# Weight sums of seven-product gate and up slices: formed in SBUF by VectorE in place of DRAM, and twelve more slices computed that way

## The chip, the cores and the metric

The kernel runs on one core of a Trainium2 chip. The metric is device time of one execution in microseconds (us); the figure of a kernel is the median of its runs. Engines: PE is TensorE (matmuls), DVE is VectorE, ACT is ScalarE, POOL is GpSimd, SP issues DMAs.

## The reference

The program is one inference step of a two-layer decoder for a prompt group (1024 tokens) and a sample group (8 tokens) with d_model = 1024. Layer 0 mixes with a gated linear recurrence and memory attention, layer 1 with stick-breaking attention over a shared K/V and memory attention. What the change touches is the feed-forward net that ends each layer:

```python
def swiglu(h, w_gu, w_down):
    gate, up = jnp.split(h @ w_gu, 2, axis=-1)
    return (jax.nn.silu(gate) * up) @ w_down
...
        h = h + rmsnorm(mix, g[1])
        h = h + rmsnorm(swiglu(rmsnorm(h, g[2]), w_gu[l], w_down[l]), g[3])
```

`w_gu[l]` is 1024 x 5632 (2816 gate columns, then 2816 up columns), `w_down[l]` is 2816 x 1024. Everything is float32.

## The kernel before, in words

**Halves.** The tokens are worked in two halves: g = 0 has 512 columns (tokens), g = 1 has 520 (512 prompt tokens and the 8 samples). Activations lie transposed, features on partitions. Every weight tile of 128 columns by 512 rows (256 KB) is loaded by SP into a raw tile (`wraw`, 5 buffers), then split in two float32r parts: ACT casts the high part (L260, L542) and DVE subtracts it from the raw tile for the low part (L261, L543), both into one tile of `wspl` (5 buffers). A product takes three matmuls per 128 x 128 block: high by high, high by low, low by high. For g = 1 each matmul covers 260 tokens.

**Feed-forward.** It has 22 slices of 128 gate and 128 up columns, in five parts of 5, 5, 4, 4 and 4 slices (`PARTS`). After the slices of a part come the eight down projections over that part (4 or 5 row blocks each), added up in a tile R. `ffn` (L688) runs three of the four feed-forward nets, among them `f1`, layer 0's second half: per slice two calls of `proj` (L266), one for gate and one for up, each 8 row blocks x 3 matmuls x 2 token halves = 48 matmuls of 260 columns. `proj` takes its PSUM tile from `mmp`, which has two buffers of two banks. SiLU is there built from Exp and Ln (`silu`, L284).

**Seven products.** The last stage of the program is `ffn_w` (L615), layer 1's second half. Its first four slices are plain (`gate_up_q`, L499). The other 18 run through `gate_up_w` (L524): gate and up weights and the two token halves form a 2 x 2 block product, which is computed with seven products of half size in place of eight. A product is 4 row blocks x 3 = 12 matmuls, a slice 84. Three of the seven weights are blocks of `w_gu`; the other four are sums of blocks:

- s1 = a21 + a22, s3 = a11 + a21, s2 = s3 + a22, s4 = s2 + a12 (a11, a12: upper and lower 512 rows of the gate columns; a21, a22: the same of the up columns).

The sums of the token side are formed once by `sums_w` (L326). In a slice, four PSUM tiles pa, pb, pc, pd are chained: product 0 goes to pa, ACT copies its negative to pb (L559); product 1 goes to pd; product 2 adds to pb, ACT copies its negative to pc (L562); product 3 adds to pa (gate of the first half, Silu at L565); product 4 adds to pb, and DVE adds pd's copy to it (L570); product 5 adds to pc, and DVE subtracts (L572); product 6 adds to pb, which is up of the first half. Two multiplications (L575, L576), a cast (L281) and a subtraction (L282) make the slice's `m` tile. In `ffn_w` the PSUM pool `quads` holds two sets of four banks, and `spl` (L624) takes three of every eight split tiles from `cpool` beside `wspl`.

**The sums before.** `weight_sums` (L588) forms s1 to s4 of layer 1 in DRAM, part by part, with 40 DMAs on POOL's queue, 16 of them beside parts 0 and 1 of `f1` and the others beside parts 2 to 4 of `f1`. Each waits for a small copy on ACT (L602) and one on POOL (L603), which tie it to the progress of `f1`. In the last stage each slice loads seven tiles of 256 KB: three from `w_gu`, four from the DRAM sums.

**Order.** The program is written as generators that `weave` interleaves by weights; the tile framework then orders each engine's instructions by its own planning and gives buffers and waits. An engine runs its instructions in that order. `f1`'s parts 0 and 1 are woven with the attention of `b0`; parts 2 to 4 run with the sums alone; then come the output projection of layer 1 (`o0`), the shared K/V, the attention of the second half, and the last stage.

Of the kernel before, what the change touches and what calls it, by code (L numbers as in the profile page):

```python
# [2 lines left out]

# [6 lines left out]
F32 = mybir.dt.float32  # L10
F32R = mybir.dt.float32r
# [7 lines left out]
P = 128  # L19
# [5 lines left out]
def tile_decoder(  # L25
# [46 lines left out]
    def nm(s):  # L72
        uid[0] += 1
        return f"{s}_{uid[0]}"
# [12 lines left out]
    def Q(i):  # L87
        return single[0].tile([P, 512], F32, tag=f"q{i}", name=nm("q"))
# [234 lines left out]
            out.append(x)  # L323
            yield

    def sums_w(xs, ops):  # L326

        n, h = NG[1], PW[1]  # L330
        for k in range(4):
            x0, x1 = xs[k], xs[k + 4]
            y = YT()
            if k % 2 == 0:
                z, u = YT(), YT()
            o = (k % 2) * h

            def full(x, c):
                t = B()
                nc.vector.tensor_add(t[:, :h], x[:, 0, c : c + h].bitcast(F32), x[:, 1, c : c + h].bitcast(F32))  # L340
                return t

            b11, b12, b21, b22 = full(x0, 0), full(x0, h), full(x1, 0), full(x1, h)
            for d, p, a, b in (
                (b11, u[:, :, o : o + h], b12, b11), (b12, y[:, :, h : 2 * h], b12, b22),
                (b22, y[:, :, :h], b22, b11), (b21, z[:, :, o : o + h], b21, b22),
            ):
                nc.vector.tensor_sub(d[:, :h], a[:, :h], b[:, :h])
                split_to((p[:, 0, :], p[:, 1, :]), d[:, :h])
            ops.append([  # L350
                x0[:, :, :h], x1[:, :, :h], x1[:, :, h:n], z[:, :, o : o + h], u[:, :, o : o + h],
                y[:, :, :h], y[:, :, h : 2 * h],
            ])
            yield

    def YT():
        return xpool.tile([P, 2, NG[1]], F32R, tag="x0", name=nm("y"))

    def wo_tiles(g):
# [161 lines left out]
        split_to((mt[:, 0, :n], mt[:, 1, :n]), sg[:, :n])  # L521
        return mt, last

    def gate_up_w(l, f, ops, spl, raws):  # L524

        h, n = PW[1], NG[1]
        part, o = part_of(f)
        gate, up = f * P, DFF + f * P
        src = [
            (w_gu[l][0:512, gate : gate + P], 0), (sums[l][part][0][:, o : o + P], 4), (sums[l][part][1][:, o : o + P], 5),  # L530
            (w_gu[l][512:D, gate : gate + P], 1), (sums[l][part][2][:, o : o + P], 6), (sums[l][part][3][:, o : o + P], 2),
            (w_gu[l][512:D, up : up + P], 3),
        ]

        def weight(j):
            r = raws()
            nc.sync.dma_start(r, src[j][0].rearrange("(k p) m -> p k m", p=P))
            return r.rearrange("p k m -> p (k m)")

        def split(src):  # L540
            w = spl()
            nc.scalar.copy(w[:, 0, :], src)  # L542
            nc.vector.tensor_sub(w[:, 1, :], src, w[:, 0, :].bitcast(F32))  # L543
            return w

        def product(ps, j, first=False):
            w = split(weight(j))
            i = src[j][1]
            for k in range(4):
                x = ops[k][i]  # L550
                for wi, (wj, xi) in enumerate(((0, 0), (0, 1), (1, 0))):
                    nc.tensor.matmul(  # L552
                        ps[:, :h], w[:, wj, k * P : (k + 1) * P], x[:, xi, :],
                        start=(first and k == 0 and wi == 0), stop=(k == 3 and wi == 2), skip_group_check=True,
                    )

        pa, pb, pc, pd = (Q(i) for i in range(4))
        product(pa, 0, True)
        nc.scalar.activation(pb[:, :h], pa[:, :h], AF.Copy, scale=-1.0)  # L559
        product(pd, 1, True)  # L560
        product(pb, 2)
        nc.scalar.activation(pc[:, :h], pb[:, :h], AF.Copy, scale=-1.0)  # L562
        product(pa, 3)
        sg = T()
        nc.scalar.activation(sg[:, :h], pa[:, :h], AF.Silu)  # L565
        product(pb, 4)
        dt = T()
        nc.scalar.copy(dt[:, h:n], pd[:, :h])
        gt = T()
        nc.vector.tensor_add(gt[:, h:n], dt[:, h:n], pb[:, :h])  # L570
        product(pc, 5)
        nc.vector.tensor_sub(gt[:, :h], pc[:, :h], dt[:, h:n])  # L572
        product(pb, 6)
        nc.scalar.activation(sg[:, h:n], gt[:, :h], AF.Silu)
        nc.vector.tensor_mul(sg[:, :h], sg[:, :h], pb[:, :h])  # L575
        nc.vector.tensor_mul(sg[:, h:n], sg[:, h:n], gt[:, h:n])  # L576
        mt = M(F32R)
        split_to((mt[:, 0, :n], mt[:, 1, :n]), sg[:, :n])
        return mt

    sums = {}

    def part_of(f):
        for i, (f0, nf) in enumerate(PARTS):
            if f0 <= f < f0 + nf:
                return i, (f - f0) * P

    def weight_sums(l, parts, after):  # L588

        for i in parts:  # L590
            f0, nf = PARTS[i]
            w = nf * P
            s1, s2, s3, s4 = (tc.dram_tile([512, w], F32, name=nm("wsum")) for _ in range(4))
            sums.setdefault(l, {})[i] = (s1, s2, s3, s4)
            a11, a12 = (w_gu[l][r : r + 512, f0 * P : f0 * P + w] for r in (0, 512))
            a21, a22 = (w_gu[l][r : r + 512, DFF + f0 * P : DFF + f0 * P + w] for r in (0, 512))
            for d, a, add in (
                (s3, a11, False), (s1, a21, False), (s3, a21, True), (s1, a22, True),
                (s2, s3, False), (s2, a22, True), (s4, s2, False), (s4, a12, True),
            ):  # L600
                tok = small([P, 1], tag="rr")
                nc.scalar.copy(tok, after())  # L602
                mark = nc.gpsimd.tensor_copy(small([P, 1], tag="mk", bufs=1), tok)  # L603
                with tc.issue_after(mark.ins):
                    if add:
                        nc.gpsimd.dma_start(d, a, accum_op=ALU.add)
                    else:
                        nc.gpsimd.dma_start(d, a, max_dma_last_dim=4 * w)
                yield

    htok = []

# [2 lines left out]
    class ffn_w:  # L615


        def __init__(self, l, x, plain):
            self.g, self.l, self.x, self.ops, self.plain, self.n, self.r, self.pi = 1, l, x, [], plain, 0, 0, 0
            self.R = self.acc = None  # L620
            self.half = []
            self.sums = sums_w(x, self.ops)

        def spl(self):  # L624
            self.n += 1
# [2 lines left out]
            return wspl.tile([P, 2, 512], F32R, tag="ws", name=nm("ws"))  # L628

        def raws(self):  # L630
            self.r += 1
            if self.pi and self.r % 2:
                if not self.half:
                    t = apool.tile([P, 2, 4, P], F32, tag="a", name=nm("w"))
                    self.half = [t[:, 0], t[:, 1]]
                return self.half.pop(0)
            return wraw.tile([P, 4, P], F32, tag="w", name=nm("w"))

        def part(self, pi):
            l, n, h = self.l, NG[1], PW[1]  # L640
# [3 lines left out]
            for j in range(nf):  # L644
                self.pi = pi
                if f0 + j < self.plain:
                    mt, ins = gate_up_q(l, f0 + j, self.x)
                    mids.append(mt)
                    with tc.issue_after(ins.ins):
                        for _ in range((1, 2, 1, 0)[j]):  # L650
                            next(self.sums, None)
                else:
                    mids.append(gate_up_w(l, f0 + j, self.ops, self.spl, self.raws))
                yield
            if pi == 0:
                self.R = R_one()
# [29 lines left out]
            yield from finish_rows(self)  # L686

    class ffn:  # L688
        def __init__(self, g, l, xt, rows=False):
            self.g, self.l, self.xt, self.rows = g, l, xt, rows  # L690
            self.R = self.acc = None

        def part(self, pi):
            g, l = self.g, self.l
# [2 lines left out]
            last = pi == len(PARTS) - 1  # L697
            mids = []
            for j in range(nf):
                pg = proj(g, w_gu[l], 0, ND, (f0 + j) * P, self.xt)  # L700
                sg = silu(None, pg, g)
                pu = proj(g, w_gu[l], 0, ND, DFF + (f0 + j) * P, self.xt)
# [1 line left out]
                mt = M(F32R)  # L704
                split_to((mt[:, 0, :n], mt[:, 1, :n]), sg[:, :n])
                mids.append(mt)
                self.now = sg[:, 0:1]
                yield
            if pi == 0:
                self.R = R_one()  # L710
            if last:
                self.acc = small([P, WID], tag="st", bufs=3)
            for m in range(ND):
                ps = proj(g, w_down[l], f0, nf, m * P, mids)
                evac_raw(g, self.R, ps, m, self.acc, pi == 0, last)
                self.now = self.R[m][:, 0:1]
                if last and self.rows:
                    nc.scalar.activation(
                        self.R[m][:, :n], self.R[m][:, :n], AF.Copy, scale=gcol(l, 3, m)
# [1 line left out]
                    if m == 3:  # L721
                        first_half(self)
                if m % 2:
                    yield

        def finish(self, store):
# [770 lines left out]
    b0 = mixer_b(0, xb0)  # L1497
    weave((b0.heads(), 8), (o1.finish(), 17))
    b0.open()
    f1 = ffn(1, 0, o1.x)  # L1500
    ws = weight_sums(1, range(5), lambda: f1.now)
    weave((chain(b0.sb(), b0.mem()), 24), (chain(f1.part(0), f1.part(1)), 18), (islice(ws, 16), 17))
    weave((chain(f1.part(2), f1.part(3), f1.part(4)), 24), (ws, 24))
    xk1, xb1 = [], []
    o0 = out_proj(0, 1, M)
    drain(o0.mm(b0.xo, 0, 1))
# [52 lines left out]
```

## Time and profile before

| what | value |
|---|---|
| median of 3 runs | 2497.13 us (2494.14 to 2497.49) |
| profiled execution: its time, its span | 2499.1 us, 2497.4 us |
| DVE, ACT, POOL busy, share of the span | 63%, 47%, 4% |
| DMA on SP's queue, on POOL's queue | 301.08 MB, 54.53 MB |
| TensorE's mean granted clock | 0.997 |

The profile's views are read so: the page gives busy time per engine; the chain of waits follows what ended last back from the end; the windows give each engine's busy time in a stretch; the timeline lists instructions with start and duration in us; groups give the mean of one instruction in ns and what ended the idle time ahead of it. A line number is that of the kernel before.

### The profile page before, as it was taken

The page shows a single profiled execution, that of the slowest core. Times are in us where ns is not written, and L with a number is a line of the kernel's source. Part 1 is how long each engine was busy: PE and PEld are TensorE (multiplying, and loading weights), DVE is VectorE, ACT ScalarE, POOL GpSimd, SP SyncE. Part 2 cuts the span into 40 slices and gives each one's busy share as a digit, 9 for nine tenths or more (in the row PEclk, how much of TensorE's full clock was granted, in tenths as well). Part 3 has the DMA queues.
Part 4 walks back from the last instruction along what each step waited for, and adds up shares of the span by engine and source line. Part 5 has one row for each costly group of instructions (what it writes and reads, how often), then busy time and mean ns, then how long its engine had stood idle before and what let it go on. Part 6 is the DMA issues. An engine that isn't in the chain of part 4 may idle for free.

```text
span 2497.4 us, 40764 instructions
## 1 busy us (share of the span) xinstructions
PE 2462.8 (99%) x15565; PEld 2169.9 (87%) x15565; DVE 1571.8 (63%) x2756; ACT 1183.0 (47%) x2277; POOL 98.3 (4%) x139
## 2 busy tenths in 40 slices
PE   8999999999999999999999999999999999999998
PEld 6888988877877897999999989877787797999997
DVE  5766556655765585655544575777577648755655
ACT  5446543243433454555433454555444445564444
POOL 1000000000000000010111100022000000000000
PEclk9999999999999999999999999999999999999999
DMA  5352252233643447586678976544454234365542
GB/s 186 114 165 68 72 156 81 60 110 116 184 124 98 129 138 227 156 195 177 173 191 215 234 193 196 160 142 138 121 149 130 85 115 122 121 192 145 151 137 69
DMA packets 496110, 358.21 MB, mean 143 GB/s; under 512 B 19110, under 2 KB 443635, under 8 KB 495915
## 3 DMA queue, kind: packets, MB, share of 16 engines
q1 hardware_dynamic: 477354, 301.08, 40.5%
q0 software_dynamic: 18560, 54.53, 9.1%
q8 instruction: 122, 2.00, 0.3%
q14 instruction: 74, 0.60, 0.1%
HBM read 325.73 MB, written 75.94 MB: 161 GB/s over the span
## 4 chain that ended last, share of the span: by engine, by line
PE 88%; DVE 5%; DMA 3%; ACT 2%; issue 2%; POOL 0%; SPq 0%; DVEq 0%; ACTq 0%; POOLq 0%
PE mm L274 59%; PE q L552 7%; PE q L667 5%; PE s L1180 2%; PE q L510 2%; PE mm L1048 2%; PE s L903 1%; PE s L862 1%; PE mm L812 1%; DMA b<-qd 1%; PE mm L839 1%; DVE ws L261 1%; PE ns L957 1%; PE s L1336 1%; DMA c<-in_cache_sb_v,pidx 1%
## 5 line engine op out<-in xcount | busy, mean ns | idle before, releaser
L274 PE MATMUL mm<-x,ws 128*128 128x260 f32 (+1 forms) x7776 | 1332.9, 330 | 0.0
L274 PEld LDWEIGHTS mm<-x,ws 128*128 128x128 f32 x7776 | 1148.3, 188 | 151.5 <-issue 12.0
L260 ACT CAST ws<-w 128x512 fp32r<-128x512 f32 x712 | 420.2, 591 | 763.2 <-PE mm L274 620.2
L261 DVE TENSOR_TENSOR ws<-w,ws 128x512 fp32r<-128x512 f32 x712 | 462.5, 653 | 286.8 <-ACT ws L260 278.3
L274 PE MATMUL mm<-m,ws 128*128 128x512 f32 (+1 forms) x2112 | 393.5, 343 | 0.1
L274 PEld LDWEIGHTS mm<-m,ws 128*128 128x128 f32 x2112 | 324.4, 189 | 49.9 <-issue 2.6
L667 PE MATMUL q<-m,ws 128*128 128x260 f32 x1056 | 128.8, 283 | 0.0
L667 PEld LDWEIGHTS q<-m,ws 128*128 128x128 f32 x1056 | 127.2, 188 | 0.4 <-ACT hT L485 0.2
L543 DVE TENSOR_TENSOR ws<-w,ws 128x512 fp32r<-128x512 f32 x126 | 86.6, 691 | 61.5 <-ACT ws L542 59.3
L552 PE MATMUL q<-y,ws 128*128 128x260 f32 x864 | 112.9, 283 | 0.0
L542 ACT CAST ws<-w 128x512 fp32r<-128x512 f32 x126 | 78.0, 621 | 69.6 <-PE q L667 27.4
L552 PEld LDWEIGHTS q<-y,ws 128*128 128x128 f32 x864 | 107.6, 189 | 0.0
L291 DVE TENSOR_SCALAR t<-mm 128x512 f32<-128x512 f32 (+1 forms) x82 | 56.7, 692 | 79.6 <-PE mm L274 79.6
L447 DVE TENSOR_TENSOR r<-r,mm 128x512 f32<-128x512 f32 (+1 forms) x96 | 66.0, 688 | 61.1 <-PE mm L274 60.3
L703 DVE TENSOR_TENSOR t<-t,mm 128x512 f32<-128x512 f32 (+1 forms) x66 | 45.5, 690 | 74.2 <-PE mm L274 73.9
L295 DVE TENSOR_TENSOR t<-t,t 128x512 f32<-128x512 f32 (+1 forms) x66 | 45.8, 694 | 70.6 <-ACT t L294 70.6
L552 PE MATMUL q<-x,ws 128*128 128x260 f32 x648 | 86.3, 282 | 0.0
L552 PEld LDWEIGHTS q<-x,ws 128*128 128x128 f32 x648 | 81.3, 188 | 0.0
L314 DVE TENSOR_TENSOR st<-st,n 128x512 f32<-128x512 f32 (+1 forms) x98 | 67.1, 691 | 8.8 <-ACT n L313 7.0
L281 ACT CAST m<-t 128x512 fp32r<-128x512 f32 (+1 forms) x88 | 54.9, 624 | 18.1 <-DVE t L703 8.9
L282 DVE TENSOR_TENSOR m<-t,m 128x512 fp32r<-128x512 f32 (+1 forms) x88 | 61.0, 693 | 2.6 <-ACT m L281 1.4
L984 POOL DMA_INDIRECT c<-in_cache_sb_k,pidx x16 | 16.4, 1026 | 1170.5 <-ACT n L313 958.6
(339 smaller groups left out, 2557.9 us busy)
## 6 DMA issues: line engine op xcount, KB each, us to landing
w<-in_w_gu SPq DMA_DIRECT2D x334, 256.0 KB, 3.4
w<-in_w_down SPq DMA_DIRECT2D x160, 256.0 KB, 3.5
w<-in_w_in_a SPq DMA_DIRECT2D x80, 256.0 KB, 3.0
wsum<-in_w_gu POOLq DMA_DIRECT2D x18, 1024.0 KB, 9.5
w<-wsum SPq DMA_DIRECT2D x72, 256.0 KB, 3.8
w<-in_w_o SPq DMA_DIRECT2D x64, 256.0 KB, 2.8
wsum<-in_w_gu POOLq DMA_DIRECT2D x12, 1280.0 KB, 10.7
w<-in_w_mem_kv SPq DMA_DIRECT2D x32, 256.0 KB, 3.2
```

The source lines that it names most:

```text
L260: nc.scalar.copy(ws[:, 0, :n, :], raw[:, :n, :])
L261: nc.vector.tensor_sub(ws[:, 1, :n, :], raw[:, :n, :], ws[:, 0, :n, :].bitcast(F32))
L274: nc.tensor.matmul(ps[:, a, : PW[g]], wt, xt[k][:, xi, o : o + PW[g]], start=(k == 0 and wi == 0), stop=(k == nk - 1 and wi == 2),)
L281: nc.scalar.copy(dst[0], src)
L282: nc.vector.tensor_sub(dst[1], src, dst[0].bitcast(F32))
L291: nc.vector.tensor_scalar(sv(x, g), pv(ps, g), -44.0, None, op0=ALU.max)
L314: nc.vector.tensor_add(acc[:, :n], acc[:, :n], t[:, :n])
L447: nc.vector.tensor_add(dst, dst, pv(ps, g))
L542: nc.scalar.copy(w[:, 0, :], src)
L543: nc.vector.tensor_sub(w[:, 1, :], src, w[:, 0, :].bitcast(F32))
L552: nc.tensor.matmul(ps[:, :h], w[:, wj, k * P : (k + 1) * P], x[:, xi, :], start=(first and k == 0 and wi == 0), stop=(k == 3 and wi == 2), ...
L667: nc.tensor.matmul(pp[a][:, :h], wt, mids[k][:, xi, a * h : (a + 1) * h], start=(k == 0 and wi == 0), stop=(k == nf - 1 and wi == 2),)
```

## The change

The DRAM sums go, with their DMAs and the small copies. A slice loads two tiles of 512 KB, one with all 1024 rows of its gate columns and one with those of its up columns (`sums_here`), and DVE forms the four sums of 128 x 512 in SBUF, into `wraw` tiles. In `ffn_w` the raw tiles come from `apool` (from `cpool` in part 0). In `f1` the slices from 10 on, twelve in parts 2 to 4, run through `gate_up_w` too: raw tiles from `cpool` (4 buffers), split tiles from `wspl` (5), and the four PSUM tiles from the two buffers of `mmp` (pa and pd in one, pb and pc in the other). `sums_w` for them is woven into the down projections of part 1 with tiles of `apool`. Silu needs another ACT table than the rest of that stage, so a table load stands ahead of the first such slice and one behind the last.

```diff
+    def sums_here(l, f, raws, outs):
+        cols = []
+        for m0 in (f * P, DFF + f * P):
+            r = raws()
+            nc.sync.dma_start(
+                r.rearrange("p a (k m) -> p (a k) m", m=P), w_gu[l][:, m0 : m0 + P].rearrange("(k p) m -> p k m", p=P)
+            )
+            cols.append(r)
+        (a11, a12), (a21, a22) = ((r[:, 0, :], r[:, 1, :]) for r in cols)
+        kept = {}
+
+        def add(a, b):
+            t = outs()
+            nc.vector.tensor_add(t, a, b)
+            return t
+
+        def weight(j):
+            if j == 1:
+                return add(a21, a22)
+            if j == 2:
+                kept[3] = add(a11, a21)
+                kept[2] = add(kept[3], a22)
+                return kept[2]
+            if j == 4:
+                return kept[3]
+            if j == 5:
+                return add(kept[2], a12)
+            return (a11, None, None, a12, None, None, a22)[j]
+
+        return weight
+
-    def gate_up_w(l, f, ops, spl, raws):
+    def gate_up_w(weight, ops, spl, quads):
...
-        def weight(j):
-            r = raws()
-            nc.sync.dma_start(r, src[j][0].rearrange("(k p) m -> p k m", p=P))
-            return r.rearrange("p k m -> p (k m)")
...
-        pa, pb, pc, pd = (Q(i) for i in range(4))
+        pa, pb, pc, pd = quads()
...
-    def weight_sums(l, parts, after):
...
     class ffn_w:
...
         def raws(self):
-            self.r += 1
-            if self.pi and self.r % 2:
-                if not self.half:
-                    t = apool.tile([P, 2, 4, P], F32, tag="a", name=nm("w"))
-                    self.half = [t[:, 0], t[:, 1]]
-                return self.half.pop(0)
-            return wraw.tile([P, 4, P], F32, tag="w", name=nm("w"))
+            if self.pi:
+                return apool.tile([P, 2, 512], F32, tag="a", name=nm("w"))
+            return C()
...
     class ffn:
-        def __init__(self, g, l, xt, rows=False):
+        def __init__(self, g, l, xt, rows=False, prod=NF):
...
+            self.sums = sums_w(xt, self.ops, lambda: A(F32R))
+
+        def quads(self):
+            ta, tb = (mmp.tile([P, 2, 512], F32, tag="mm", name=nm("mm")) for _ in range(2))
+            return ta[:, 0, :], tb[:, 0, :], tb[:, 1, :], ta[:, 1, :]
...
             for j in range(nf):
+                if f0 + j >= self.prod:
+                    mt, gate = gate_up_w(
+                        sums_here(l, f0 + j, C, lambda: wraw.tile([P, 512], F32, tag="w", name=nm("w"))),
+                        self.ops, lambda: wspl.tile([P, 2, 512], F32R, tag="ws", name=nm("ws")), self.quads,
+                    )
+                    mids.append(mt)
+                    yield
+                    continue
...
+            if last and self.prod < NF:
+                with tc.issue_after(gate.ins):
+                    nc.scalar.preload_act_table_set("natural_log_exp_and_others")
...
                 if m % 2:
+                    if f0 + nf == self.prod < NF:
+                        next(self.sums, None)
                     yield
...
-    f1 = ffn(1, 0, o1.x)
-    ws = weight_sums(1, range(5), lambda: f1.now)
-    weave((chain(b0.sb(), b0.mem()), 24), (chain(f1.part(0), f1.part(1)), 18), (islice(ws, 16), 17))
-    weave((chain(f1.part(2), f1.part(3), f1.part(4)), 24), (ws, 24))
+    f1 = ffn(1, 0, o1.x, prod=10)
+    weave((chain(b0.sb(), b0.mem()), 24), (chain(f1.part(0), f1.part(1)), 18))
+    drain(f1.part(2), f1.part(3), f1.part(4))
```

More of the change, by code (lines that the diff above doesn't have):

```diff
@@ L1 @@
 from contextlib import ExitStack
-from itertools import islice
 import concourse.bass as bass
@@ L324, in normed, with sums_w @@
             yield
-    def sums_w(xs, ops):
+    def sums_w(xs, ops, YT):
         n, h = NG[1], PW[1]
@@ L354, in sums_w, with Y0 @@
             yield
-    def YT():
+    def Y0():
         return xpool.tile([P, 2, NG[1]], F32R, tag="x0", name=nm("y"))
@@ L522, in gate_up_q @@
         return mt, last
-    def gate_up_w(l, f, ops, spl, raws):
-        h, n = PW[1], NG[1]
[L527 to L533, printed above, removed]
-        def weight(j):
-            r = raws()
-            nc.sync.dma_start(r, src[j][0].rearrange("(k p) m -> p k m", p=P))
-            return r.rearrange("p k m -> p (k m)")
+    def sums_here(l, f, raws, outs):
[26 more added lines that the diff above has]
+    def gate_up_w(weight, ops, spl, quads):
+        h, n = PW[1], NG[1]
+        src = (0, 4, 5, 1, 6, 2, 3)
         def split(src):
@@ L547, in product @@
             w = split(weight(j))
-            i = src[j][1]
+            i = src[j]
             for k in range(4):
@@ L573, in gate_up_w @@
         product(pb, 6)
-        nc.scalar.activation(sg[:, h:n], gt[:, :h], AF.Silu)
+        last = nc.scalar.activation(sg[:, h:n], gt[:, :h], AF.Silu)
         nc.vector.tensor_mul(sg[:, :h], sg[:, :h], pb[:, :h])
@@ L578, in gate_up_w @@
         split_to((mt[:, 0, :n], mt[:, 1, :n]), sg[:, :n])
[L579 to L586, printed above, removed]
-    def weight_sums(l, parts, after):
[L590 to L609, printed above, removed]
+        return mt, last
     htok = []
@@ L618, in __init__ @@
         def __init__(self, l, x, plain):
-            self.g, self.l, self.x, self.ops, self.plain, self.n, self.r, self.pi = 1, l, x, [], plain, 0, 0, 0
+            self.g, self.l, self.x, self.ops, self.plain, self.n, self.pi = 1, l, x, [], plain, 0, 0
             self.R = self.acc = None
-            self.half = []
-            self.sums = sums_w(x, self.ops)
+            self.sums = sums_w(x, self.ops, Y0)
         def spl(self):
@@ L652, in part @@
                 else:
-                    mids.append(gate_up_w(l, f0 + j, self.ops, self.spl, self.raws))
+                    mids.append(gate_up_w(
+                        sums_here(l, f0 + j, self.raws, lambda: wraw.tile([P, 512], F32, tag="w", name=nm("w"))),
+                        self.ops, self.spl, lambda: [Q(i) for i in range(4)]
+                    )[0])
                 yield
@@ L688, in tile_decoder @@
     class ffn:
-        def __init__(self, g, l, xt, rows=False):
-            self.g, self.l, self.xt, self.rows = g, l, xt, rows
+        def __init__(self, g, l, xt, rows=False, prod=NF):
+            self.g, self.l, self.xt, self.rows, self.prod = g, l, xt, rows, prod
             self.R = self.acc = None
+            self.ops = []
+            self.sums = sums_w(xt, self.ops, lambda: A(F32R))
+        def quads(self):
+            ta, tb = (mmp.tile([P, 2, 512], F32, tag="mm", name=nm("mm")) for _ in range(2))
+            return ta[:, 0, :], tb[:, 0, :], tb[:, 1, :], ta[:, 1, :]
         def part(self, pi):
@@ L706, in part @@
                 mids.append(mt)
-                self.now = sg[:, 0:1]
                 yield
+            if last and self.prod < NF:
+                with tc.issue_after(gate.ins):
+                    nc.scalar.preload_act_table_set("natural_log_exp_and_others")
             if pi == 0:
@@ L715, in part @@
                 evac_raw(g, self.R, ps, m, self.acc, pi == 0, last)
-                self.now = self.R[m][:, 0:1]
                 if last and self.rows:
```

## The prediction

> **What bounds the kernel now.** First I read the page's header and its busy times, then the chain of waits, then PE's waits, then the windows of the stages that the change touches.
>
> ```profile
> span 2497.4 us, 40764 instructions
> ...
> PE 2462.8 (99%) x15565; PEld 2169.9 (87%) x15565; DVE 1571.8 (63%) x2756; ACT 1183.0 (47%) x2277; POOL 98.3 (4%) x139
> ```
>
> ```profile
> 1241.31 209.76 PE mm L274 x1730
> ...
> 1463.78 7.70 DMA w<-in_w_o
> ...
> 2415.18 40.35 PE q L552 x336
> ```
>
> PE is busy for 99% of the span, and in the chain parts 2 to 4 of `f1` are one piece of matmuls without a gap (1241.31 to 1451.07). Four seven-product slices of the last stage are one piece too: 336 matmuls in 40.35 us are 0.120 us each. In the long piece 1730 take 209.76 us, 0.121 each. So a matmul of 260 columns costs 0.120 us in either stage, and what removes one there shortens the span, unless PE then has to wait.
>
> ```profile
> 1200.00:1215.00 15.00, 15.00 (x113) 14.18 (x112) 8.03 (x19) 6.12 (x18) 0.99 (x2) 1.00 0.84 222
> 1215.00:1230.00 15.00, 15.00 (x115) 14.52 (x114) 8.36 (x17) 6.80 (x18) 1.35 (x2) 1.00 0.90 195
> 1241.31:1451.07 209.76, 209.76 (x1731) 208.73 (x1731) 104.84 (x153) 84.49 (x154) 31.10 (x48) 1.00 0.84 214
> 2288.44:2328.78 40.34, 40.34 (x338) 40.34 (x338) 26.60 (x48) 24.32 (x50) 0.00 (x0) 1.00 0.63 181
> ```
>
> After the length come PE, weight load, DVE, ACT and POOL busy, then clock, DMA share and GB/s. DVE has half its time free in `f1` (104.84 of 209.76) and a third free in the seven-product slices (26.60 of 40.34). The clock is 1.00 everywhere here, so it plays no part.
>
> **The change, part by part.** All terms are changes of the profiled execution's 2499.1 us.
>
> *Fewer matmuls.* Twelve slices go from 96 to 84 matmuls: 144 x 0.120 = **-17.3 us**. This term is as sure as PE staying fed.
>
> *New waits at each slice boundary of `f1`.* The spacing of instructions is read from the timeline of the last stage, where the same instructions already run.
>
> ```profile
> 2308.45 1.59 PE L552 MATMUL q<-x,ws 128*128 128x260 f32 x12
> 2309.88 3.06 PE L552 MATMUL q<-y,ws 128*128 128x260 f32 x24
> ```
>
> ```profile
> 2309.30 0.69 DVE L543 TENSOR_TENSOR ws<-w,ws 128x512 fp32r<-128x512 f32 x1
> 2309.91 0.70 DVE L282 TENSOR_TENSOR m<-t,m 128x520 fp32r<-128x520 f32 x1
> ...
> 2316.28 0.42 DVE L570 TENSOR_TENSOR t<-t,q 128x260 f32<-128x260 f32 x1
> 2316.62 0.69 DVE L543 TENSOR_TENSOR ws<-w,ws 128x512 fp32r<-128x512 f32 x1
> ```
>
> ```profile
> 2310.08 0.37 ACT L559 ACTIVATE q<-q 128x260 f32<-128x260 f32 x1 [0.20 <-PE q L552]
> ...
> 2118.85 0.62 ACT L281 CAST x<-n 128x520 fp32r<-128x520 f32 x1
> 2119.36 0.63 ACT L305 ACTIVATE st<-st 128x512 f32<-128x512 f32 x1
> ```
>
> A 512-element DVE instruction takes DVE 0.61 us from start to start (2309.30 to 2309.91; a weight sum has the same shape and I give it the same), a 260-element one 0.34 with its result after 0.42. A 512-element cast takes ACT about 0.55 (0.51 here). A consumer starts 0.20 after PE has issued the last matmul that it needs (2309.88 to 2310.08). A product is 12 x 0.120 = 1.44 us of PE.
>
> In the changed kernel's order PE issues, after product 4 of a slice: 8 matmuls of the next slice's product 0, then 5, the other 4 of product 0, 6, the next 1, the next 2. That is 0.96 + 1.44 + 0.48 + 1.44 + 1.44 = 5.76 us until the next product 2. That one writes pb, so ACT must have copied -pa there, and DVE must have multiplied the old pb out of it, because both slices use one PSUM buffer. DVE's order at the first two boundaries of a part is, from 0.57 us on (it has a split before): add, split, two weight sums, subtraction, the third sum, split, multiplication, split, and the multiplication that frees pb: 0.57 + 0.34 + 0.61 + 1.22 + 0.34 + 0.61 + 0.61 + 0.34 + 0.61 + 0.42 = 5.67. Then ACT's queue holds the cast of `m` (0.55) ahead of the copy (0.37), with 0.1 for hand-overs: 6.69. PE waits **0.9 us**. At the third boundary DVE has no sums (1.83 less), but then the wait for product 5 and its successors holds: 2.39 + 0.20 (cast 0.62, split 0.61, multiplication 0.34, split 0.61, multiplication 0.42, cast 0.55, copy 0.37, hand-overs) = 6.2: **0.5 us**. Into the down projection the second PSUM buffer is late by **0.3 us**. Three parts: 3 x (0.9 + 0.9 + 0.5 + 0.3) = **+7.8 us**. Before, `proj` had no such loop. Bounds: 3, if DVE and ACT run each of the ten steps 0.05 faster; 15, if every step lost another 0.06. I take 7.8, worked from the rows above. DVE's total is no limit: a slice holds 11 x 0.61 + 4 x 0.34 + 0.61 = 8.7 us beside 10.1 us of PE.
>
> By the Trainium skill (Perfetto Trace Analysis, Optimization Strategy), the same gap repeating along a stretch can mean too little SBUF or PSUM for the next tile; by that rule the gap would be there in `f1` with four banks and absent in the last stage with eight. The last stage's row of 40.34 us busy in 40.34 agrees for the eight; no run here shows the four.
>
> *Larger loads, and DVE waiting for them.* The sums stand in DVE's queue ahead of the gate add, so a late load holds all behind them.
>
> ```profile
> w<-in_w_gu SPq DMA_DIRECT2D x334, 256.0 KB, 3.4
> ...
> c<-in_cache_mem_k SPq DMA_DIRECT2D x16, 512.0 KB, 3.9
> ...
> ht<-in_x_prompt SPq DMA_DIRECT2D x8, 512.0 KB, 5.5
> ...
> wsum<-in_w_gu POOLq DMA_DIRECT2D x12, 1280.0 KB, 10.7
> ```
>
> The last figure is us from issue to landing. A 512 KB load of 512-byte runs does not occur before. I take 4.2: nearest to the 512 KB row of 3.9; bounds 3.4 and 5.5. In `f1` a raw tile is free after the split of its slice's product 6, some 2.8 us ahead of the next boundary, and the sums are due 1.5 us behind it, so 4.2 just fits. In the last stage split tiles run seven or eight products ahead and most sums find their load landed; only in the fourth part does a load start as late as the slice's own start. There: issue 1.7, landing 5.9, five DVE instructions of 0.61, the add of 0.42: 9.4 us, where product 6 wants 8.6. **+0.8**, and 0.5 for smaller waits at four or five other slices: **+1.3 us**, bounds 0 and 9 (six slices with 1.3 us more each, at 5.5). DVE's load there rises by 16 x 0.61 = 9.8 us per four slices, to 36.4 of 40.34: near full, not over.
>
> The Trainium skill (DMA: Bandwidth & Descriptors, Anatomy of one DMA) fits a DMA as about 2.0 us plus bytes over 436 GB/s. For 512 KB that estimate is 3.2 us, and the sum would lose this 1.3 and be 1.3 us lower. The row of 3.9 for the same size lies above it, so the sum keeps the row.
>
> *Token sums of layer 0.* 16 additions, 16 subtractions and 16 low parts of 260 elements are 48 x 0.34 = 16.3 us on DVE, and 16 casts on ACT, beside the end of part 1. DVE is 55% busy there (8.03 and 8.36 of 15 us); over the 36 us in which they stand that makes 20 + 16 = 36, full. The splits run ahead of PE, so I take **+1.0 us**, bounds 0 and 4.
>
> *Table loads.*
>
> ```profile
> L517 ACT ACT_TABLE_LOAD x1 | 1.3, 1283 | 0.0
> ```
>
> Two more, 1.28 us of ACT each. The first falls where ACT has slack; the second stands ahead of the last slice's cast: **+0.3 us**, bounds 0 and 2.6.
>
> *The DRAM sums go.* POOL's DMAs and the small copies cost PE little: in the windows above it is busy throughout beside them. They do delay loads: the chain has 7.70 us of waiting for `in_w_o` just behind them, with PE at other work, and at its end this wait:
>
> ```profile
> PE ns L303 <- DVE st L314: 1.5, 2, 1.2
> ```
>
> I take **-1.3 us**, bounds 0 and -1.5. The work that follows is ordered anew by the framework; its PE waits before are so small that I give it 0, within 3 us either way.
>
> *Sum.* -17.3 + 7.8 + 1.3 + 1.0 + 0.3 - 1.3 = **-8.2 us**: 2490.9 for the profiled execution. That one was 2.0 us above the median of 2497.1, so the median becomes **2489 us**.
>
> **The rivals.**
>
> *All waits hidden.* PE gains 17.3 and the DMA relief, and the splits' lead covers the rest: 2497.1 - 17.3 - 1.3 + 1 = 2479.5. For it: before, PE hardly waits anywhere. Against: the copy to pb has no lead, it needs the old slice's last product.
>
> *Late loads make it slower.* DVE stands at a sum that waits for its 512 KB, and the gate add and the freeing of pb stand behind it. About twelve slices are open to this (six in `f1`, six in the last stage). Each us of landing beyond 4.2 costs 12 us, so from 4.2 + 8.2/12 = 4.9 us on the kernel is slower. At the 5.5 of the `ht` row: 2489 + 12 x 1.3 = 2504.6. For it: that row has the same size. Against: it was taken beside POOL's DMAs, which are gone.
>
> *Bubbles eat the gain.* If each of the nine inner boundaries of `f1` cost 1.7 instead of 0.9 or 0.5, that is 8.7 us more: 2497.6, no change to speak of. For it: DVE's chain of ten instructions leaves nothing to spare. Against: the spacings come from the same instructions at work.
>
> **How the numbers follow.** A measurement of this kernel tells about 0.2%, 5 us, from no change. Forecast, 2483 to 2495: 0.50. All hidden: 0.15. Late loads: 0.17. Bubbles: 0.18. The forecast's case is faster by over 0.2% in 0.42 of its 0.50 and within it in 0.08. The hidden case is faster. The bubbles split 0.01 faster, 0.15 same, 0.02 slower. The late loads are 0.02 same, 0.15 slower. So faster 0.58, same 0.25, slower 0.17. The range reaches to the hidden case's 2479 and into the late loads, to 2503.
>
> **What would show it.** Matmuls in the twelve slices fall by 144. Windows over parts 2 to 4 of `f1` should be about 199 us, with PE idle or matmuls stretched some 0.5 to 0.9 us at each product 2, released by ACT's copy, whose own wait is for DVE. In the last stage PE's piece per four slices should stay near 40.4 us, with one of the parts 1 us longer. A landing of over 4.9 us for the `w_gu` loads, or DVE idle for DMA at the weight sums, would speak for the late loads. The prediction is wrong if the stretch of parts 2 to 4 is near 190 or over 205 us, or if the time moves elsewhere.

## The result, and the profile after

The median of six runs is 2518.3 us (2516.09 to 2522.69), against 2497.31 us before; the ratio is 1.0087, 95% interval 1.0074 to 1.0100. The change makes the kernel slower by 21 us, where the forecast was 2489, that is 8 us faster, and 2503 was the upper end of the range. The profiled execution took 2518.8 us, with a span of 2517.1.

The head of the page of the changed kernel:

```profile
span 2517.1 us, 40253 instructions
...
PE 2460.4 (98%) x15421; PEld 2157.6 (86%) x15421; DVE 1670.4 (66%) x2972; ACT 1202.5 (48%) x2315; POOL 45.5 (2%) x59
```

PE has 144 matmuls fewer, but its busy time falls by 2.4 us only, and the span grows by 19.7. (A matmul counts as busy until its modelled end, so part of a wait hides in the busy time.)

Where the stages end is read from the chain of waits. Of the kernel before, the start of the last stage; of the changed one, the end of `f1`, the start of the last stage, and DMAs on which the end hung:

```profile
2115.33 2.03 PE q L510 x15
```

```profile
1436.56 26.53 PE mm L273 x198
...
2125.49 2.03 PE q L509 x15
...
2175.51 5.56 DMA c<-in_w_gu
2181.09 1.30 DVE w L536 x2
...
2228.23 3.85 DMA w<-in_w_gu
...
2445.76 4.65 DMA w<-in_w_gu
```

`f1`'s matmuls end at 1463.09 where they ended at 1451.07: +12.0. The last stage begins at 2125.49 where it began at 2115.33: +10.2, so the stretch between won back 1.9. From there to the end of the span it is 391.6 us where it was 382.1: +9.5. In sum 12.0 - 1.9 + 9.5 = 19.6 of the 19.7. (From here on the end of `f1` is read at the first matmul of L302 behind it, which starts at 1450.9 before and at 1462.9 in the changed kernel.)

PE's waits in the changed kernel (engine, line that waits and what it waits for; us in total, times, longest):

```profile
PE mm L571 <- ACT mm L578: 16.1, 12, 1.7
...
PE q L571 <- ACT ws L561: 2.9, 2, 1.6
...
PE q L571 <- DVE t L589: 1.8, 3, 1.3
...
PE ns L302 <- DVE st L313: 0.3, 1, 0.3
```

The first row is new and large: twelve times, once per slice, PE stood before a product of `f1` until ACT's copy of -pa to pb (L578) was done. The last row answers to the 1.5 us of before. Windows of the changed kernel (length; PE, weight load, DVE, ACT and POOL busy; clock, DMA share, GB/s): `f1` from its first seven-product slice to its end, the seven-product slices of the third, fourth and fifth part of the last stage, and a piece of part 1 of `f1`:

```profile
1235.49:1462.92 227.43, 208.09 (x1622) 199.04 (x1621) 150.69 (x255) 101.80 (x201) 7.88 (x8) 1.00 0.37 110
2307.91:2348.28 40.37, 40.37 (x339) 40.37 (x338) 30.87 (x56) 23.93 (x49) 0.00 (x0) 1.00 0.45 131
2371.26:2412.22 40.96, 40.62 (x339) 40.41 (x338) 29.50 (x53) 23.70 (x49) 0.00 (x0) 1.00 0.49 142
2435.56:2476.41 40.85, 40.63 (x338) 40.42 (x338) 29.16 (x53) 23.74 (x49) 0.00 (x0) 1.00 0.27 78
...
1215.00:1230.00 15.00, 15.00 (x115) 14.49 (x114) 15.00 (x40) 8.43 (x22) 0.00 (x0) 1.00 0.05 13
```

The clock is 1.00 in all of them, as before. `f1` loses some 19 us of PE's time to idleness. The last stage's four-slice pieces take 40.37, 40.96 and 40.85 us, where 40.34, 40.37 and 40.35 were before: 1.1 us more. The first part, up to its last down projection, is 7.7 us longer (101.55 in place of 93.81, up to 2227.04 and 2209.14), the second 1.6; behind the fifth part's slices the program ends 1.2 us sooner (40.7 in place of 41.9), for which no run gives the reason.

**The boundary of two slices in `f1`.** PSUM is the memory that matmuls write to; a tile of `mmp` spans two of its banks. The timelines of PE, ACT and DVE in the changed kernel, around one boundary. The sums of the token side are the tiles named `a` there (products 1, 2, 4 and 6), the halves are `x` (products 0, 3 and 5):

```profile
1259.35 1.60 PE L571 MATMUL mm<-a,ws 128*128 128x260 f32 x12
1260.79 3.23 PE L571 MATMUL mm<-x,ws 128*128 128x260 f32 x24
1264.07 1.71 PE L571 MATMUL mm<-a,ws 128*128 128x260 f32 x12
1267.48 3.17 PE L571 MATMUL mm<-a,ws 128*128 128x260 f32 x24 [1.70 <-ACT mm L578]
```

```profile
1259.84 0.37 ACT L587 COPY t<-mm 128x260 f32<-128x260 f32 x1
...
1266.52 0.63 ACT L280 CAST m<-t 128x520 fp32r<-128x520 f32 x1
1267.05 0.37 ACT L578 ACTIVATE mm<-mm 128x260 f32<-128x260 f32 x1
```

```profile
1263.59 0.43 DVE L591 TENSOR_TENSOR t<-mm,t 128x260 f32<-128x260 f32 x1
...
1266.08 0.41 DVE L594 TENSOR_TENSOR t<-t,mm 128x260 f32<-128x260 f32 x1
```

Read from below: DVE multiplies the old pb out at 1266.08, as the tenth of its chain. ACT casts `m`, then copies -pa to pb at 1267.05. PE has ended product 6 (from 1264.07, 1.44 us of issue) at 1265.5 and goes on at 1267.48, with 24 matmuls on `a` tiles. These are product 1 and product 2 of the next slice in one piece. So it is product 1 that waits for the copy, not product 2. Product 1 writes pd, and pd lies in one PSUM tile with pa, which the copy reads. The old pd was no hindrance: ACT had copied it out at 1259.84 (L587). From one such group to the next it is 12.58 us (1254.90 to 1267.48; 12.4 at the third boundary of a part), where 84 matmuls at 0.120 are 10.08. A plain slice of before takes 96 x 0.121 = 11.6: with its waits the slice of seven products was longer than the one of eight.

**The first seven-product slice of the last stage.** SP issues its DMAs one after another, and one that waits holds those behind it, as the rows below show. SP's timeline of the changed kernel, SP's wait, and DVE's timeline:

```profile
2146.42 0.97 SPq L527 DMA_DIRECT2D c<-in_w_gu  x1
2174.19 1.26 SPq L1460 DMA_DIRECT2D out_y_prompt<-c  x2
2175.51 0.46 SPq L527 DMA_DIRECT2D c<-in_w_gu  x1
```

```profile
SPq L1460 <- DVE c L1458: 28.3, 2, 26.7
```

```profile
2181.09 0.69 DVE L536 TENSOR_TENSOR w<-c 128x512 f32<-128x512 f32 x1 [4.77 <-DMA c<-in_w_gu]
```

The load of the gate columns went out at 2146.42, that of the up columns 29 us later. Between them stand two stores of output rows, which waited 28.3 us on SP's queue (26.7 the longer) for copies that follow PE's transposes. The second load landed at 2181.1, after DVE had stood idle for 4.77 us. Product 1 needs the up columns; PE started the slice at 2175.65 and came to product 1 at 2182.49.

### The profile page after: what moved, and what is told of

It is laid out like the page before. It is cut to its first block, busy times and chain, and to the rows that moved or that the text cites. A ratio compares the mean times of both kernels' runs of the same rounds, so it can differ in the third digit from the quotient of the medians.

```text
span 2517.1 us, 40253 instructions
## 1 busy us (share of the span) xinstructions
PE 2460.4 (98%) x15421; PEld 2157.6 (86%) x15421; DVE 1670.4 (66%) x2972; ACT 1202.5 (48%) x2315; POOL 45.5 (2%) x59
## 5 line engine op out<-in xcount | busy, mean ns | idle before, releaser
L273 PE MATMUL mm<-x,ws 128*128 128x512 f32 (+1 forms) x6624 | 1193.6, 338 | 0.0
L273 PEld LDWEIGHTS mm<-x,ws 128*128 128x128 f32 x6624 | 1009.4, 188 | 152.3 <-issue 12.2
L259 ACT CAST ws<-w 128x512 fp32r<-128x512 f32 (+1 forms) x664 | 390.5, 589 | 665.4 <-PE mm L273 525.3
L260 DVE TENSOR_TENSOR ws<-w,ws 128x512 fp32r<-128x512 f32 (+1 forms) x664 | 428.8, 649 | 271.4 <-ACT ws L259 262.5
L561 ACT CAST ws<-w 128x512 fp32r<-128x512 f32 x171 | 105.5, 621 | 85.4 <-PE q L654 25.1
L562 DVE TENSOR_TENSOR ws<-w,ws 128x512 fp32r<-128x512 f32 x171 | 116.9, 687 | 28.7 <-ACT ws L561 27.6
L571 PE MATMUL mm<-a,ws 128*128 128x260 f32 x576 | 78.3, 288 | 17.9 <-ACT mm L578 16.1
L571 PEld LDWEIGHTS mm<-a,ws 128*128 128x128 f32 x576 | 71.7, 188 | 22.7 <-ACT mm L578 18.6
L290 DVE TENSOR_SCALAR t<-mm 128x512 f32<-128x512 f32 (+1 forms) x70 | 48.3, 690 | 61.7 <-PE mm L273 61.5
L704 DVE TENSOR_TENSOR t<-t,mm 128x512 f32<-128x512 f32 (+1 forms) x54 | 37.1, 688 | 56.6 <-PE mm L273 55.9
```

What stands on the lines that cost most here:

```text
L259: nc.scalar.copy(ws[:, 0, :n, :], raw[:, :n, :])
L260: nc.vector.tensor_sub(ws[:, 1, :n, :], raw[:, :n, :], ws[:, 0, :n, :].bitcast(F32))
L273: nc.tensor.matmul(ps[:, a, : PW[g]], wt, xt[k][:, xi, o : o + PW[g]], start=(k == 0 and wi == 0), stop=(k == nk - 1 and wi == 2),)
L290: nc.vector.tensor_scalar(sv(x, g), pv(ps, g), -44.0, None, op0=ALU.max)
L571: nc.tensor.matmul(ps[:, :h], w[:, wj, k * P : (k + 1) * P], x[:, xi, :], start=(first and k == 0 and wi == 0), stop=(k == 3 and wi == 2), ...
```

## The experiments

Theory A for `f1`: the tile that pa and pd share, and the reuse of pb, make the wait. Its rival, theory B: five split tiles are too few, and the weights would be late whatever the banks. For the last stage, theory A: the queue position of the second load; its rival, theory C: the length of a 512 KB load, or DVE's fullness.

### pd in a tile of its own (e1_pd_apart)

```diff
-            return ta[:, 0, :], tb[:, 0, :], tb[:, 1, :], ta[:, 1, :]
+            return ta[:, 0, :], tb[:, 0, :], tb[:, 1, :], S()
```

> Only pd of the twelve slices of f1 moves out of the tile that it shares with pa, into a PSUM tile of its own; the work is the same. Theory A (PE waits at product 1, not at product 2, because pd lies in the tile that the copy of -pa reads): product 1 runs ahead of the copy, product 2 waits about 0.9 us as forecast; PE's waits for the copy in f1 fall from 16.1 us to about 8, the inner slices from 12.6 us to about 11.1, nine of them: 2518.3 - 13 = 2505, range 2500 to 2508. Theory B (five split tiles are too few: the weights of products 1 and 2 come no earlier, whatever the banks): the wait goes over to the casts and subtractions of weights (L561, L562), at most 0.5 us a slice is won: 2513 or more.

Measured: 2503.39 us (2500.11 to 2505.56) beside 2498.35 for before, ratio 1.0018 (1.0009 to 1.0028). PE's waits for the copy and its timeline at a boundary:

```profile
PE mm L571 <- ACT mm L578: 4.1, 10, 0.5
```

```profile
1252.34 1.71 PE L571 MATMUL mm<-a,ws 128*128 128x260 f32 x12 [0.50 <-ACT mm L578]
...
1263.47 1.72 PE L571 MATMUL mm<-a,ws 128*128 128x260 f32 x12 [0.52 <-ACT mm L578]
```

Only product 2 waits now (a group of 12), and a slice takes 11.13 us (1252.34 to 1263.47; 10.95 at the third boundary of a part). `f1` ends at 1444.8, 18.2 us earlier. Theory B is out: the weights were there. The forecast had 0.9 us at the first two boundaries of a part, that is 10.08 + 0.9 = 10.98, and 0.5 at the third.

### All four tiles apart (e2_all_apart)

```diff
-            ta, tb = (mmp.tile([P, 2, 512], F32, tag="mm", name=nm("mm")) for _ in range(2))
-            return ta[:, 0, :], tb[:, 0, :], tb[:, 1, :], ta[:, 1, :]
+            ta, td = (mmp.tile([P, 2, 512], F32, tag="mm", name=nm("mm")) for _ in range(2))
+            return ta[:, 0, :], S(), S(), td[:, 0, :]
```

pa and pd stand in the two tiles of `mmp`, pb and pc in the three small banks that the attention leaves free. In this kernel the gate and up values that are added up in pb and pc come out other than the reference's; it issues the same matmuls. (pb and pc begin with ACT's copy, and no matmul starts a sum in them. By the Trainium skill, PSUM — Partial Sum Buffer, The four PSUM rules, a matmul that does not start a sum adds only where an earlier matmul left a status bit set, and overwrites elsewhere; the attention used these banks last, with 128 to 256 columns. Which columns were overwritten, no run here shows.)

> All four PSUM tiles of the twelve slices of f1 are tiles of their own, pb and pc from the three small banks that the attention leaves free. Theory A (shared tiles and the reuse of pb cost f1 its 29 us): waits of PE in f1 fall under 4 us, a slice takes 10.1 to 10.5 us, f1 ends 24 to 29 us earlier: 2489 to 2494, below the kernel before by 3 to 8 us. Theory B (split tiles): PE still idles over 15 us in f1, now released by L561 and L562; 2505 or more.

Measured: 2494.57 us (2492.7 to 2495.98), ratio 0.9983 (0.9974 to 0.9993), 0.6 above the range. PE's timeline at two boundaries (product 5 of one slice, and of the next):

```profile
1258.39 1.60 PE L571 MATMUL s<-x,ws 128*128 128x260 f32 x12
...
1268.49 1.60 PE L571 MATMUL s<-x,ws 128*128 128x260 f32 x12
```

A slice takes 10.10 us, which is 84 matmuls at 0.120: no wait is left between slices. `f1` ends at 1437.4, 25.6 us earlier than in the changed kernel. Of the 29.3 us that it lost (12.0 later, where 17.3 earlier was due), 18.2 went with pd's tile and 7.4 more with the rest of the shared or reused banks. (PE's order is another too: the seven products of a slice now follow each other, with no matmuls of the next slice between them, so the 7.4 belong to both.) Of the 3.7 that are left, 0.8 is a wait of the attention for L883 and 0.8 one of the first slice for L589; the rest is not explained.

### The last stage's loads one slice earlier (e3_early_load)

```diff
+                if pi == 0 and j == 3:
+                    early = sums_here(l, f0 + 4, self.raws, lambda: wraw.tile(...))
...
-                        sums_here(l, f0 + j, self.raws, lambda: wraw.tile(...)),
+                        early if pi == 0
+                        else sums_here(l, f0 + j, self.raws, lambda: wraw.tile(...)),
```

> The two 512 KB loads of the last stage's first seven-product slice are issued one slice earlier, ahead of the output stores in SP's queue; all else as in the changed kernel. Theory A (the second load waits in SP's queue behind two output stores that wait for copies, issue at 2175.5 where the first went at 2146.4): PE's waits at that slice go, 2518.3 - 7.5 = 2511, range 2509 to 2512.5. Theory C (a 512 KB load lands in over 5 us and the sums wait for it wherever it stands, or DVE is full there): a gain under 2 us, 2516.5 or more.

Measured: 2509.93 us (2508.35 to 2511.14), ratio 1.0043 (1.0029 to 1.0058): 8.4 us below the changed kernel. SP's queue and PE's first seven-product slice there:

```profile
2125.57 19.74 SPq L254 DMA_DIRECT2D w<-in_w_gu  x8
2164.49 8.77 SPq L254 DMA_DIRECT2D w<-in_w_down  x4
2173.56 0.95 SPq L1463 DMA_DIRECT2D out_y_prompt<-c  x2
```

```profile
2172.95 1.68 PE L571 MATMUL q<-x,ws 128*128 128x260 f32 x12
2174.47 3.06 PE L571 MATMUL q<-y,ws 128*128 128x260 f32 x24
2177.36 1.60 PE L571 MATMUL q<-x,ws 128*128 128x260 f32 x12
```

No gate or up load stands behind the stores any more, and the products follow each other without a gap. The last stage takes 384.3 us (2124.44 to 2508.7) in place of 391.6. The same loads of 512 KB, issued in time, cost nothing: theory C is out for this slice.

### The last stage alone (e4_last_only)

```diff
-    f1 = ffn(1, 0, o1.x, prod=10)
+    f1 = ffn(1, 0, o1.x)
```

> f1 runs with plain products, as before the change; the last stage keeps the sums in SBUF. If the loss is the sum of two stages that do not act on each other (f1 +12.0, the stretch between -1.9, last stage +9.5): 2497.3 - 1.9 + 9.5 = 2505, range 2503 to 2507, and the last stage's waits are those of the changed kernel. If the late loads of the last stage come from what f1 shifts: near 2496.

Measured: 2507.84 us (2506.86 to 2510.26), ratio 1.0040 (1.0025 to 1.0054), 0.8 above the range. `f1` ends at 1451.2, the stretch behind it takes 0.9 us less than before, the last stage 390.4 us, 8.4 more. Its chain has the same late load:

```profile
2165.20 5.58 DMA c<-in_w_gu
```

So the last stage's loss does not come from `f1`. The stretch between the stages is 0.9 us shorter than before here and 1.9 in the changed kernel, but it scatters by more than that: it takes 664.4 us before, 665.4 in e1 and 660.5 in the second profile of the changed kernel below.

### Both mends (e5_apart_early, e6_pairs_early, e7_apart_early2)

e5 takes the loads of e3 and, in `f1`, own tiles for all four; its first two slices take the small banks for pa and pd, whose first matmul starts a sum over all 260 columns (shown beside e2):

```diff
+            self.k = getattr(self, "k", 0) + 1
             ta, td = (mmp.tile([P, 2, 512], F32, tag="mm", name=nm("mm")) for _ in range(2))
+            if self.k < 3:
+                return S(), ta[:, 0, :], td[:, 0, :], S()
             return ta[:, 0, :], S(), S(), td[:, 0, :]
```

> Both mends together: in f1 all four PSUM tiles are tiles of their own (the first two slices take the small banks for pa and pd and whole tiles of mmp for pb and pc, the other ten the small banks for pb and pc), and the last stage's first seven-product slice has its loads issued one slice earlier. If the two causes are separate, the gains add up: 2518.3 - 23.7 (all four apart) - 8.4 (early loads) + 1 (pb of the second slice still uses the first's bank) = 2487, range 2484 to 2490. If the early loads of the last stage only take the place of another wait once f1 ends earlier: 2492 or more.

Measured: 2489.53 us (2488.37 to 2491.63), ratio 0.9961 (0.9947 to 0.9975). The gains add up to the 2487 that was expected, less 2.5 us. A new wait of that size stands in the tail of the attention:

```profile
PE s L899 <- DVE b L889: 2.5, 1, 2.5
```

e6 leaves pb and pc in one tile, of which successive slices take turns with two buffers:

```diff
+            t = mmp.tile([P, 2, 512], F32, tag="mm", name=nm("mm"))
+            return S(), t[:, 0, :], t[:, 1, :], S()
```

> As the run beside it, but pb and pc of f1 still share one tile, of which two slices take turns with two buffers; pa and pd have small banks of their own. Two waits stay that only the shared tile makes: product 5 for the addition that reads pb (L589), product 6 for the subtraction that reads pc (L591). If what costs is the reuse of pb and the tile that pa and pd share, these two cost under 0.3 us a slice, since four or eight matmuls of the next slice stand between: 2486 to 2491. If any sharing of a tile costs as much as that of pa and pd (1.4 us a slice): 2487 + 12 x 1.4 = 2504.

Measured: 2493.65 us (2491.87 to 2495.87), ratio 0.9983 (0.9974 to 0.9993): 4.1 above e5, or 0.34 us a slice, where under 0.3 was expected and 1.4 by the rival; the time is 2.7 above the range. Its timeline shows a slice of 10.35 us (product 5 at 1263.15 and at 1273.50):

```profile
1263.15 1.71 PE L571 MATMUL mm<-x,ws 128*128 128x260 f32 x12
...
1273.50 1.72 PE L571 MATMUL mm<-x,ws 128*128 128x260 f32 x12
```

So in these two cases a shared tile costs what the other use of it is late by: 1.45 us where it put the copy's wait a whole product earlier (12.58 to 11.13), 0.3 where a reader on DVE comes soon behind.

e7 adds to e5 that the first slice of the last stage's second part takes its raw tiles from `cpool`, issued in the first part, and that this slice takes no split tiles from there:

```diff
-            if self.pi and self.n % 8 in (1, 4, 6):
+            if self.pi and self.n > 14 and self.n % 8 in (1, 4, 6):
...
+                self.next = sums_here(l, f0 + nf, C, lambda: wraw.tile(...))
...
+                        early if pi == 0 else self.next if pi == 1 and j == 0
```

> As the first run of this call, and the first slice of the last stage's second part takes its raw tiles from cpool and is issued in the first part, ahead of the release of the tiles that the sample rows hold until 2211.8. If that release is what makes PE wait 1.9 us there: 2487 - 1.8 = 2485, range 2482 to 2488; if the wait is DVE's own work there, the same as the first run.

Measured: 2487.21 us (2484.06 to 2487.59), ratio 0.9951 (0.9934 to 0.9968), 2.3 below e5, where 1.8 was expected. The wait of 1.7 us for L589 at that slice is gone: of PE's waits for L589 in the last stage (2.2 us in e5) 0.7 is left. The last stage takes 382.6 us (2099.64 to 2482.2), where it took 382.1 before, 391.6 in the changed kernel and 384.3 in e3: with both edits it has its old length.

### The first slice of f1 with one small bank (e8_apart_early3), and the changed kernel again (e9_f1_only)

Shown beside e7:

```diff
+            if self.k == 1:
+                return ta[:, 0, :], td[:, 0, :], td[:, 1, :], S()
-            if self.k < 3:
+            if self.k < 4:
                 return S(), ta[:, 0, :], td[:, 0, :], S()
```

> As e7_apart_early2, but the first slice of f1, which still runs beside the end of the attention, takes only one of the three small banks (for pd) in place of two. If PE's 2.5 us of waiting at 1237.4 (a transpose of the attention, for a DVE result) comes from the two small banks taken away from the attention: that wait goes, 2487.2 - 2.3 = 2485, range 2483 to 2487. If it comes from DVE's weight sums at that place: no change, 2487 to 2489.

Measured: 2482.21 us (2480.45 to 2486.05), ratio 0.9936 (0.9922 to 0.9949), 0.8 below the range. This is the fastest version here, 16 us under the kernel before and 36 under the changed one. The attention's wait of 2.5 us is gone, but `f1` ends at 1436.1 as in e7 (1436.0), and the two ratios' intervals overlap. The two profiles do not run level up to that point, though. One group of attention matmuls just ahead of `f1`'s seven products, first in e7, then in e8:

```profile
1230.95 1.02 PE L914 MATMUL s<-b,c 128*128 128x256 f32 x4
```

```profile
1233.71 1.02 PE L916 MATMUL s<-b,c 128*128 128x256 f32 x4
```

e7's was 2.8 us ahead there; in e5, which has the same `f1` as e7, it starts at 1233.67. From this group to the end of `f1` it is 202.4 us in e8, 205.1 in e7 and 206.4 in e5. So the stretch is 2.6 to 4.0 us shorter, where 2.3 was expected; with one profile of each, and 1.3 us between two of the same code, only the sign of this is clear.

The other label holds the changed kernel unaltered:

> The changed kernel once more, beside the other run on one chip: 2516 to 2522 by its six times. A second profile of it shows how much the stages scatter: f1 to its end 1462.9, the last stage 391.6 us, each within 1.5 us.

Measured: 2517.09 us, with `f1` ending at 1462.9 and a last stage of 392.0 us. The end of `f1` and the last stage of the changed kernel repeat within half a microsecond; the stretch between them differs by 2.1.

## Why the prediction was wrong, point by point

**Fewer matmuls, -17.3: right.** 15565 to 15421 on the page, and in e2 a slice takes 10.10 us, which is 84 x 0.120.

**Waits at the boundaries of f1, +7.8: this step failed, and it made most of the miss.** In place of 7.8 us `f1` lost 29.3, and the stretch of parts 2 to 4, which was to be about 199 us and a sign of error from 205 on, took 221.8 (209.76 + 12.0). The prediction had the wait at product 2, with the next product 1 running ahead of it ("5.76 us until the next product 2"). It had worked out when the copy would be done, and this came nearly true: with pd apart (e1) the slices take 11.13 us where 10.98 follows from it, and `f1` loses 11.1 us in all. What was overlooked is that pd stands in pa's tile. Therefore product 1 waits for the copy too, and no longer hides 1.44 us of it: 0.9 + 1.44 = 2.3 of the 2.5 measured at the first two boundaries of a part. Taken as 2.5, 2.5 and 2.3 in each of three parts, the nine boundaries make 21.9 us. The other 7.4 of 29.3 fell at the first slice of each part and ahead of the down projections. Two pieces of it are waits of PE behind a weight sum whose load was late, 1.23 us at 1249.24 and 1.28 at 1324.74; in e1 both are gone. The upper bound of 15 was made by lengthening the steps of the chain; no bound was made for a wrong place of the wait. The rival of the bubbles named these boundaries, with 1.7 us each, but by the length of DVE's chain and not by a shared tile, and it stopped at no change. (Its 8.7 us more are 8.4 by its own figures: 6 x 0.8 + 3 x 1.2.)

The Trainium skill (Perfetto Trace Analysis, Optimization Strategy) says that a gap that repeats can mean too little SBUF or PSUM for the next tile. The trace agrees: the gap of 1.5 to 1.7 us came at nine boundaries of two shared tiles, and with more banks (e2) it is gone. But for pd it was not room: its bank had been read out 7.3 us before product 1 wrote it (1260.21 and 1267.48), and what product 1 waited for was the reader of pa.

**Larger loads, +1.3: the step failed for two slices, and was right for the rest.** The last stage lost 9.5 us. The third part of the last stage took 40.37 us for four slices, the fourth 40.96 and the fifth 40.85, which is 1.1 us more than before and near the 1.3. Landing, from the issue to the sum, was 5.56, 3.85 and 4.65 us in the three cases on the chain, around the 4.2 taken. The failure was in "In the last stage split tiles run seven or eight products ahead and most sums find their load landed". That looked at the raw tiles and passed over what stands ahead of the load in SP's queue (first slice: the 7.3 us that e3 took from the last stage) and who else still holds the tile (first slice of the second part: 1.3 us of waiting in the changed kernel, 1.7 in e5, which e7 took away). Nor did most sums find their load landed. DVE's idle time (us, times) ahead of the weight sums of the changed kernel, by the load that ended it:

```profile
  DMA w<-in_w_gu: 11.1, 8
  DMA c<-in_w_gu: 8.2, 3
```

Nine of these eleven times lie in the last stage, which has 18 such slices, but PE lost little by most of them.

The Trainium skill (DMA: Bandwidth & Descriptors, Anatomy of one DMA) gave an estimate of 3.2 us for 512 KB, from a fit that the page makes for DMAs issued by gpsimd. These loads go out on SP's queue, and the three landings here, 3.85 to 5.56 us, all lie above it.

**Token sums of layer 0, +1.0: nothing.** DVE is busy for 15.00 of the 15 us from 1215 on, as forecast, and PE too. A group of attention matmuls at the end of part 1 starts at 1233.52 where it started at 1233.51 before.

**Table loads, +0.3: nothing to be seen.** Beside the second one (L711), PE has product 6 and the down projections.

**The DRAM sums, -1.3: not told from the scatter.** PE's wait for L314 of 1.5 us is 0.3. But the stretch behind `f1`, 664.4 us before, is 662.6 in the changed kernel, 660.5 in its second profile, 663.5 in e4 and 665.4 in e1, all without the DRAM sums.

**The rival on the slower side, late loads (0.17):** its sign was right, its size not. DVE did stand at a sum and wait for its 512 KB, and at eleven slices, near the twelve that it counted. But most of these waits were 0.4 to 3.1 us long and PE lost little by them. The one that cost much, 4.77 us of DVE's time in the first slice of the last stage, came of the place of the issue and not of a long landing.

## What to carry to other kernels

When two values share a tile, a writer of one can be made to wait for a reader of the other: list for each PSUM or SBUF tile all its readers and writers, and put the wait at the first writer of any part of it. A load is as late as the first instruction ahead of it in its queue that has to wait, so of each moved DMA look at what stands ahead of it in the issuing queue and at the last holder of its tile, before its length. A step that a wait covers can make a smaller count of matmuls the longer slice; here 84 with 2.5 us of waits took longer than 96 without.

## What was not expected of the hardware

DVE ran at 15.00 busy of 15 us (1215 to 1230) while PE was busy for 15.00 as well: a full vector engine alone cost PE nothing in this window.
